# Global attention: row sums added ahead of the context tiles' scaling, and transposed behind the third pair of key tiles

## The chip, the cores and the metric

One core of a Trainium2 chip runs the whole kernel. The metric is the device time of one execution in microseconds (us), as the median of several runs. The engines are TensorE (PE for its matmuls, PEld for its weight loads), VectorE (DVE), ScalarE (ACT), GpSimd (POOL) and SyncE (SP), which issues most DMAs here.

## The reference

One transformer layer over 1024 latent tokens of width 1024, with 256 context tokens that serve as further keys. Two attention branches read the same input; what the change touches is the second, global one: 8 query heads in 2 groups of 4, each over all 1024 latent keys and the 256 context keys in one softmax.

```python
def _global_attention(q, k_all, v_all):
    def one_block(i):
        q_blk = lax.dynamic_slice_in_dim(q, i * BLOCK, BLOCK, axis=1)      # 128 queries
        p = jax.nn.softmax(_gqa_scores(q_blk, k_all), axis=-1)
        return _gqa_values(p, v_all)
...
    o_a = _windowed_attention(q_a, k_a, v_a, k_a_c, v_a_c, sink)
    o_b = _global_attention(q_b, concatenate([k_b, k_b_c]), concatenate([v_b, v_b_c]))
    y = (g_a * (o_a @ w_branch_a) + g_b * (o_b @ w_branch_b)) @ w_out
    x = _layer_norm(ALPHA * x + gate1 * y)
    x = _layer_norm(ALPHA * x + gate2 * _conv_ffn(x * (1 + scale2) + shift2))
```

All of it is in fp32.

## The kernel before, in words

fp32 is made from pairs: `split` (L79 to L86) writes a rounded high part (L81 on ACT, L83 on POOL) and a low remainder (L86), and a product is the sum of several matmuls (`mm3`, L88 to L91).

The attention runs over 32 units, first 16 of the windowed branch and then 16 of the global one. A global unit is one block of 128 queries (`i`, 0 to 7) and one group of 4 heads (`g`, 0 or 1); this text calls the unit of block 3 and group 0 "3_0". A unit has two halves.

The score half: `cxp` multiplies the queries with the 256 context keys into one score tile (s_x; L493 and L494, a matmul for the high and one for the low part), takes the row maxima on DVE (L550), scales them by the query norms (L551, 128x4), and ACT takes the exponentials (L505) into the tile p_x and their sums into smc. `lat` does the same for each of the four heads over the 1024 latent keys: scores in s_0 to s_3 (L493, L494), row maximum and copy on DVE (L538), exponentials on ACT (L505) with the sums in sm. Two score tiles have PSUM buffers at a time. Then `norm` (L558 to L573) joins both: f = exp(difference of the maxima) (L562, L563), the four 128x256 pieces of p_x are multiplied by f on POOL (L566), smc is multiplied by f (L567), and added to sm (L568).

The value half has ten key tiles, eight latent and two context ones. `tr_step` transposes each tile's four 128x128 pieces on PE into a PSUM tile ptr_n (L613), which is split into pth and ptl: by ACT (L622) and DVE (L623), or for tiles 2 and 6 by a copy on ACT (prw, L619) and both parts on POOL (L83, L86). `av_step` multiplies them with the values into the tile av (L634, L635). The context tiles, ptr_8 and ptr_9, are the only ones that read p_x. `rows` (L575 to L589) transposes sm on PE into the tile str (L577), takes the reciprocal on DVE (L581), writes it to DRAM as dn (L586) and broadcasts it back into rb by two DMAs (L588). `out_step` copies av (L640), adds its two halves on POOL (L642, L646) and multiplies by rb (L649); the split result O is read by the branch's output matmuls (L89 to L91 on tiles b), for which raw weights rwb are loaded and split into hwb and lwb (L83, L86 on POOL, L1028 for the last ones).

`value_steps` lists the steps of a unit's value half: five pairs of key tiles, with `rows` inserted between them (L666). The main loop (L964 to L996) interleaves the score half of unit u with the value half of unit u−1 and with pieces of the output products by a fraction for each step, and in some units adds weight sums: DMAs on SP (L682) that POOL's accumulating DMAs (L684) follow. From that list the framework's scheduler orders the instructions of each engine, so a step moved in the list can stand elsewhere among its neighbours on every engine. str, the ptr tiles, and the transposed queries qtr share three PSUM buffers in turn.

Of the kernel before, what the change touches and what calls it, by code (L numbers as in the profile page):

```python
# [10 lines left out]
ALU = mybir.AluOpType  # L11
# [57 lines left out]
def layer_kernel(  # L69
# [6 lines left out]
    nc = tc.nc  # L76
    PSUM = bass.MemoryType.PSUM

    def split(src, hi, lo, hi_eng, lo_eng):  # L79
        if hi_eng is nc.scalar:  # L80
            nc.scalar.copy(hi, src)  # L81
        elif hi_eng is nc.gpsimd:
            nc.gpsimd.tensor_scalar(out=hi, in0=src, scalar1=1.0, scalar2=0.0, op0=ALU.mult, op1=ALU.add)  # L83
        else:
            hi_eng.tensor_copy(hi, src)
        lo_eng.tensor_tensor(out=lo, in0=src, in1=hi.bitcast(F32), op=ALU.subtract)  # L86
# [376 lines left out]
    class Unit:  # L463
# [94 lines left out]
        def norm(self):  # L558
            hc = slice(self.g * 4, self.g * 4 + 4)
            f = small(f"f_{self.id}", (P, 4))  # L560
            if self.br:
                nc.vector.tensor_tensor(out=f, in0=self.nm, in1=self.other, op=ALU.subtract)  # L562
                nc.scalar.activation(f, f, AF.Exp)  # L563
                for h in range(4):
                    p = self.pc[h, 1]
                    nc.gpsimd.tensor_scalar(out=p, in0=p, scalar1=f[:, h:h + 1], scalar2=0.0, op0=ALU.mult, op1=ALU.add)  # L566
                nc.gpsimd.tensor_tensor(out=self.smc, in0=self.smc, in1=f, op=ALU.mult)  # L567
                nc.gpsimd.tensor_tensor(out=self.sm, in0=self.sm, in1=self.smc, op=ALU.add)  # L568
            else:
                nc.vector.tensor_tensor(out=f, in0=self.nm, in1=sinkb[:, hc], op=ALU.add)  # L570
                nc.scalar.activation(f, f, AF.Exp)
                nc.vector.tensor_tensor(out=self.sm, in0=self.sm, in1=f, op=ALU.add)
                nc.vector.reciprocal(self.sm, self.sm)  # L573
# [31 lines left out]
        def value_steps(self):  # L605
            nm, kt = self.id, self.kt
            vh = self.br * 2 + self.g
            parts = {}

            def tr_step(n):  # L610
                tr = pt_tile(f"ptr{nm}_{n}")
                for h in range(4):
                    nc.tensor.transpose(tr[:, h * P:(h + 1) * P], self.pslice(h, n), ident)  # L613
                hi = att.tile([P, 512], R32, tag="pth", name=f"pth{nm}_{n}", bufs=4)
                lo = att.tile([P, 512], R32, tag="ptl", name=f"ptl{nm}_{n}", bufs=4)
                pooled = n in POOL_LO[self.br]
                if pooled:
                    rw = att.tile([P, 512], F32, tag="ptr", name=f"prw{nm}_{n}", bufs=2)
                    nc.scalar.copy(rw, tr)  # L619
                    split(rw, hi, lo, nc.gpsimd, nc.gpsimd)  # L620
                else:
                    nc.scalar.copy(hi, tr)  # L622
                    nc.vector.tensor_tensor(out=lo, in0=tr, in1=hi.bitcast(F32), op=ALU.subtract)  # L623
                parts[n] = hi, lo
                return pooled

            def av_step(n):
                first = self.left == len(kt)
                self.left -= 1
                if first:  # L630
                    self.av = ps2.tile([P, 512], F32, tag="av", name=f"av{nm}")
                hi, lo = parts.pop(n)
                v = VT[kt[n] // 2][:, kt[n] % 2, vh]
                nc.tensor.matmul(self.av, v, hi, start=first, stop=False)  # L634
                nc.tensor.matmul(self.av, v, lo, start=False, stop=self.left == 0)  # L635

            def out_step():
                av = self.av
                avs = att.tile([P, 512], F32, tag="ptr", name=f"avs{nm}", bufs=2)
                nc.scalar.copy(avs, av)  # L640
                up = att.tile([HD, 512], F32, tag="up", name=f"up{nm}", bufs=1)
                nc.gpsimd.tensor_scalar(out=up, in0=avs[HD:P], scalar1=1.0, scalar2=0.0, op0=ALU.mult, op1=ALU.add)  # L642
                ot = att.tile([P, 2, P], F32, tag="ot", name=f"ot{nm}", bufs=1)
                oe = nc.gpsimd if self.br else nc.vector
                for h in range(2):
                    oe.tensor_tensor(out=ot[h * HD:(h + 1) * HD],  # L646
                                     in0=avs[0:HD].rearrange("p (a b q) -> p a b q", b=2, q=P)[:, :, h],
                                     in1=up.rearrange("p (a b q) -> p a b q", b=2, q=P)[:, :, h], op=ALU.add)
                nc.gpsimd.tensor_tensor(out=ot, in0=ot, in1=self.rb, op=ALU.mult)  # L649
                hf = self.i // 4  # L650
                qs = slice((self.i % 4) * P, (self.i % 4 + 1) * P)
                split(ot, otile(self.br, hf, 0, self.g)[:, :, qs], otile(self.br, hf, 1, self.g)[:, :, qs],
                      nc.gpsimd, nc.gpsimd)

            def step(ns):
                pooled = [tr_step(n) for n in ns]
                for n, pl in zip(ns, pooled):
                    clk[0] += 1
                    avq.append((self, n, clk[0] + LAG[self.br] + (PLAG[self.br] if pl else 0)))
                    av_issue()  # L660

            self.left = len(kt)
            self.av_step, self.out_step = av_step, out_step
            g = 1 + self.br
            steps = [lambda n=n: step(range(n, n + g)) for n in range(0, len(kt), g)]
            steps.insert(2 - self.br if self.br or self.i else len(steps), self.rows)  # L666
            return steps

    tokens = []
# [215 lines left out]
    def otile(br, hf, hl, g):  # L885
        key = br, hf, hl, g
        if key not in O:
            O[key] = opool.tile([P, 2, HALF], R32, tag="O", name="O%d%d%d%d" % key, bufs=12)
        return O[key]
# [4 lines left out]
    def pt_tile(name, dt=F32):  # L894
        return ps2.tile([P, 512], dt, tag="pt", name=name, bufs=3)
# [7 lines left out]
    def small(name, shape):  # L903
        return att.tile(list(shape), F32, tag=name.split("_")[0], name=name,
                        bufs=4)
# [4 lines left out]
    def av_issue(flush=False):  # L910
        while avq:
            u = avq[0][0]
            c = [e for e in avq if e[0] is u and (flush or e[2] <= clk[0])]
            if not c:
                return
            e = min(c, key=lambda e: e[2])
            avq.remove(e)
            u.av_step(e[1])
            if u.left == 0:
                u.out_step()  # L920
# [988 lines left out]
```

## Time and profile before

| | |
|---|---|
| median of 3 runs | 1570.69 us (1568.04 to 1571.46) |
| the profiled execution's own time | 1569.94 us |
| its span from first to last instruction | 1568.1 us |
| global attention in it | about 470 to 770 us of the span |
| granted TensorE clock | 0.997 of full speed on average |

A row of a timeline gives start, duration, engine, line, operation, the tiles written and read, and in brackets the idle time of the engine just ahead of it with the instruction that released it. A row of the list of waits gives the waiting engine and line, what it waited for, total idle time, how often, and the longest. A row of the groups gives busy time and mean duration in ns, then idle time ahead of them. Weight loads overlap matmuls, so the idle time ahead of a matmul (PE) and ahead of its weight load (PEld) differ.

### The profile page before, as it was taken

To read this page: it belongs to the slowest core of one execution; us is meant where nothing else is said; L and a number is where in the kernel's file an instruction comes from. 1 tells how busy PE (TensorE), PEld (TensorE's weight loads), DVE (VectorE), ACT (ScalarE), POOL (GpSimd) and SP (SyncE) were. 2 spreads that over 40 slices of the span, in tenths; PEclk is the share of its full clock that TensorE was granted. 3 is DMA by queue.
4 is the path that set the end of the run, shared out by engine and by line. 5 is a ranking of instruction groups with operands and counts; after the bars stand their busy time and mean duration, and the time that the engine had idled before them with its cause. 6 is when DMAs were issued, how large, how long until landed. Compare 5 with 4: busy or idle time off the path is not lost.

```text
span 1568.1 us, 22308 instructions
## 1 busy us (share of the span) xinstructions
PE 1532.0 (98%) x7804; PEld 1279.6 (82%) x7804; DVE 1192.3 (76%) x1707; ACT 811.3 (52%) x1430; POOL 783.6 (50%) x801
## 2 busy tenths in 40 slices
PE   9999999999999999999899999999999999999997
PEld 7888888888877777787688998888888888888887
DVE  6677976548888777778574789888888888657884
ACT  5323223358888777777330674544444444435552
POOL 0356423526667777677432444766677774021121
PEclk9999999999999999999999999999999999999998
DMA  9776662322236666430550223233334446996821
GB/s 371 266 242 237 210 247 84 112 81 63 65 123 149 155 156 168 105 86 17 179 176 27 82 93 107 96 108 109 118 111 111 112 115 188 367 266 209 254 103 55
DMA packets 113105, 232.11 MB, mean 148 GB/s; under 512 B 13056, under 2 KB 27904, under 8 KB 112896
## 3 DMA queue, kind: packets, MB, share of 16 engines
q1 hardware_dynamic: 97760, 201.82, 38.0%
q0 software_dynamic: 10400, 20.19, 8.3%
q10 hardware_dynamic: 4832, 8.68, 1.5%
q8 instruction: 61, 1.00, 0.3%
q14 instruction: 52, 0.43, 0.1%
HBM read 179.45 MB, written 65.86 MB: 156 GB/s over the span
## 4 chain that ended last, share of the span: by engine, by line
PE 84%; POOL 5%; DVE 4%; issue 2%; DMA 2%; ACT 2%; SPq 0%; DVEq 0%; ACTq 0%; POOLq 0%
PE ptr L613 5%; PE p L89 4%; PE p L90 4%; PE p L91 4%; PE g L89 4%; PE g L90 4%; PE g L91 4%; PE b L90 3%; PE b L91 3%; PE b L89 3%; PE s L493 2%; PE av L634 2%; PE av L635 2%; PE c L89 2%; PE c L91 2%; PE d L91 2%
## 5 line engine op out<-in xcount | busy, mean ns | idle before, releaser
L623 DVE TENSOR_TENSOR ptl<-ptr,pth 128x512 fp32r<-128x512 f32 x188 | 126.0, 685 | 46.5 <-ACT pth L622 43.5
L622 ACT CAST pth<-ptr 128x512 fp32r<-128x512 f32 x188 | 106.9, 588 | 55.4 <-PE av L634 25.9
L86 DVE TENSOR_TENSOR ld<-rd,hd 128x1024 fp32r<-128x1024 f32 x77 | 94.8, 1248 | 50.4 <-ACT hd L81 48.2
L505 ACT ACTIVATE p<-p,nm 128x1024 f32<-128x1024 f32 (+2 forms) x128 | 125.4, 981 | 12.0 <-DVE p L538 11.6
L613 PE MATMUL ptr<-ident,p 128*128 128x128 f32 x816 | 126.2, 277 | 2.3 <-DVE ptl L623 0.9
L81 ACT CAST hd<-rd 128x1024 fp32r<-128x1024 f32 x77 | 79.4, 1049 | 81.4 <-PE p L91 57.2
L613 PEld LDWEIGHTS ptr<-ident,p 128*128 128x128 f32 x816 | 94.6, 140 | 27.0 <-DVE ptl L623 6.3
L86 POOL TENSOR_TENSOR wlg<-wg,whg 128x512 fp32r<-128x512 f32 x32 | 47.2, 1486 | 123.6 <-ACT whg L81 84.4
L634 PE MATMUL av<-pth,VT 128*128 128x512 f32 x236 | 104.4, 442 | 1.7 <-POOL pth L83 1.2
L89 PE MATMUL p<-hd 128*128 128x512 f32 x264 | 103.3, 391 | 0.0
L90 PE MATMUL p<-ld,hd 128*128 128x512 f32 x264 | 102.8, 389 | 0.0
L91 PE MATMUL p<-hd,ld 128*128 128x512 f32 x264 | 102.8, 389 | 0.0
L635 PE MATMUL av<-ptl,VT 128*128 128x512 f32 x236 | 98.2, 416 | 3.1 <-POOL ptl L86 3.1
L89 PE MATMUL g<-hh,whg 128*128 128x512 f32 x256 | 99.9, 390 | 0.0
L91 PE MATMUL g<-hh,wlg 128*128 128x512 f32 x256 | 99.7, 389 | 0.0
L90 PE MATMUL g<-hl,whg 128*128 128x512 f32 x256 | 99.6, 389 | 0.0
L538 DVE TENSOR_SCALAR_CACHE_REDUCE p<-s,cvt,nmc 128x1024 f32<-128x1024 f32 x64 | 84.0, 1330 | 9.7 <-PE s L494 9.5
L493 PE MATMUL s<-KL,q 128*128 128x512 f32 (+2 forms) x192 | 75.4, 393 | 3.6 <-ACT p_x L505 1.8
L786 ACT ACTIVATE sg<-g,bgc 128x512 f32<-128x512 f32 x32 | 21.9, 686 | 96.1 <-PE g L91 91.3
L494 PE MATMUL s<-KL,q 128*128 128x512 f32 (+2 forms) x192 | 71.6, 373 | 0.0
L81 ACT CAST wS<-s 128x512 fp32r<-128x512 f32 x76 | 45.3, 621 | 47.5 <-POOL s L1211 46.8
L81 ACT CAST wA<-ru 128x512 fp32r<-128x512 f32 x57 | 35.5, 623 | 62.9 <-PE d L91 34.8
(436 smaller groups left out, 5022.8 us busy)
## 6 DMA issues: line engine op xcount, KB each, us to landing
wml<-in_wmodT_dram SPq DMA_DIRECT2D x48, 512.0 KB
ru<-in_w_up_dram SPq DMA_DIRECT2D x38, 512.0 KB
rd<-td SPq DMA_DIRECT2D x55, 256.0 KB
rd<-sd SPq DMA_DIRECT2D x44, 256.0 KB
rd<-in_w_dn_dram SPq DMA_DIRECT2D x33, 256.0 KB
wm<-in_wmodT_dram SPq DMA_DIRECT2D x16, 512.0 KB
wg<-in_w_g_dram SPq DMA_DIRECT2D x32, 256.0 KB
sgd<-sg ACTq DMA_DIRECT2D x32, 256.0 KB
```

What stands on the lines that cost most here:

```text
L81: nc.scalar.copy(hi, src)
L86: lo_eng.tensor_tensor(out=lo, in0=src, in1=hi.bitcast(F32), op=ALU.subtract)
L89: nc.tensor.matmul(ps, a[0], b[0], start=start, stop=False, skip_group_check=resumed)
L90: nc.tensor.matmul(ps, a[0], b[1], start=False, stop=False, skip_group_check=resumed)
L91: nc.tensor.matmul(ps, a[1], b[0], start=False, stop=stop, skip_group_check=resumed)
L493: nc.tensor.matmul(o, self.q[0][:, hs], ks, start=True, stop=False)
L505: nc.scalar.activation(p, s, AF.Exp, bias=nm[:, h:h + 1], scale=scale, accum_out=sm[:, h:h + 1])
L613: nc.tensor.transpose(tr[:, h * P:(h + 1) * P], self.pslice(h, n), ident)
L622: nc.scalar.copy(hi, tr)
L623: nc.vector.tensor_tensor(out=lo, in0=tr, in1=hi.bitcast(F32), op=ALU.subtract)
L634: nc.tensor.matmul(self.av, v, hi, start=first, stop=False)
L635: nc.tensor.matmul(self.av, v, lo, start=False, stop=self.left == 0)
```

## The change

In `norm` the two 128x4 operations on the row sums stand ahead of the four scalings of p_x (lines L564 and L565 of the changed kernel, the scaling is then L568). In `value_steps` the step `rows` goes behind the third pair of key tiles (ptr_4, ptr_5) for the 16 global units, where it stood behind the first pair (ptr_0, ptr_1). The windowed units keep their places, 2 or the end.

```diff
             if self.br:
                 nc.vector.tensor_tensor(out=f, in0=self.nm, in1=self.other, op=ALU.subtract)
                 nc.scalar.activation(f, f, AF.Exp)
+                nc.gpsimd.tensor_tensor(out=self.smc, in0=self.smc, in1=f, op=ALU.mult)
+                nc.gpsimd.tensor_tensor(out=self.sm, in0=self.sm, in1=self.smc, op=ALU.add)
                 for h in range(4):
                     p = self.pc[h, 1]
                     nc.gpsimd.tensor_scalar(out=p, in0=p, scalar1=f[:, h:h + 1], scalar2=0.0, op0=ALU.mult, op1=ALU.add)
-                nc.gpsimd.tensor_tensor(out=self.smc, in0=self.smc, in1=f, op=ALU.mult)
-                nc.gpsimd.tensor_tensor(out=self.sm, in0=self.sm, in1=self.smc, op=ALU.add)
...
             steps = [lambda n=n: step(range(n, n + g)) for n in range(0, len(kt), g)]
-            steps.insert(2 - self.br if self.br or self.i else len(steps), self.rows)
+            steps.insert(3 if self.br else 2 if self.i else len(steps), self.rows)
```

What the scheduler makes of it is shown at unit 3_0. The first place is on PE, where the score tile s_0 of unit 3_1 has just been multiplied. Before:

```order
L493 MATMUL s_3_1_0_6603<-KL_2133,q_3_1_6289 128x512
L494 MATMUL s_3_1_0_6603<-KL_2133,q_3_1_6290 128x512
L577 MATMUL str_3_0_6611<-ident,sm_3_0_6321 4x128
L613 MATMUL ptr_3_0_2_6633<-ident,p_3_0_0_6369 128x128
L613 MATMUL ptr_3_0_2_6633<-ident,p_3_0_1_6401 128x128
L613 MATMUL ptr_3_0_2_6633<-ident,p_3_0_2_6444 128x128
L613 MATMUL ptr_3_0_2_6633<-ident,p_3_0_3_6452 128x128
L634 MATMUL av_2_1_6436<-pth_2_1_9_6553,VT_2139 128x512
```

The same place after the change:

```order
L493 MATMUL s_3_1_0_6603<-KL_2133,q_3_1_6289 128x512
L494 MATMUL s_3_1_0_6603<-KL_2133,q_3_1_6290 128x512
L613 MATMUL ptr_3_0_2_6611<-ident,p_3_0_0_6369 128x128
L613 MATMUL ptr_3_0_2_6611<-ident,p_3_0_1_6428 128x128
L613 MATMUL ptr_3_0_2_6611<-ident,p_3_0_2_6456 128x128
L613 MATMUL ptr_3_0_2_6611<-ident,p_3_0_3_6464 128x128
L613 MATMUL ptr_3_0_3_6622<-ident,p_3_0_0_6369 128x128
```

str is gone from there, and the tiles ptr_2 and ptr_3 follow one another. The second place is where str stands on PE now, behind the last score tile s_3 of unit 3_1; before the change the pieces of ptr_5 stood around that tile:

```order
L493 MATMUL s_3_1_3_6688<-KL_2133,q_3_1_6289 128x512
L494 MATMUL s_3_1_3_6688<-KL_2133,q_3_1_6290 128x512
L577 MATMUL str_3_0_6696<-ident,sm_3_0_6321 4x128
L634 MATMUL av_3_0_6643<-pth_3_0_3_6627,VT_2136 128x512
L613 MATMUL ptr_3_0_6_6713<-ident,p_3_0_0_6369 128x128
L613 MATMUL ptr_3_0_6_6713<-ident,p_3_0_1_6428 128x128
```

Between the two places stand 16 transposes and 18 matmuls of 512 columns. The third place is POOL, around the scalings of p_x in the same unit. Before:

```order
L83 TENSOR_SCALAR hwb_3_0_6621<-rwb_3_0_6619 128x1024
L566 TENSOR_SCALAR p_3_0_x<-p_3_0_x,f_3_0_6475 128x256 x4
L567 TENSOR_TENSOR smc_3_0_6332<-smc_3_0_6332,f_3_0_6475 128x4
L86 TENSOR_TENSOR lwb_3_0_6622<-rwb_3_0_6619,hwb_3_0_6621 128x1024
L568 TENSOR_TENSOR sm_3_0_6321<-sm_3_0_6321,smc_3_0_6332 128x4
```

After:

```order
L83 TENSOR_SCALAR hwb_3_0_6648<-rwb_3_0_6646 128x1024
L564 TENSOR_TENSOR smc_3_0_6332<-smc_3_0_6332,f_3_0_6475 128x4
L568 TENSOR_SCALAR p_3_0_x<-p_3_0_x,f_3_0_6475 128x256
L565 TENSOR_TENSOR sm_3_0_6321<-sm_3_0_6321,smc_3_0_6332 128x4
L568 TENSOR_SCALAR p_3_0_x<-p_3_0_x,f_3_0_6475 128x256 x3
L86 TENSOR_TENSOR lwb_3_0_6649<-rwb_3_0_6646,hwb_3_0_6648 128x1024
```

The sum sm stands behind one of the four scalings, and the weight split lwb behind all of them. On DVE the reciprocal of the unit moves from behind ptl_1 to behind ptl_5, ahead of the row maximum that reads s_2 of the next unit. On SP the dn write and the two broadcasts move with it; in the last unit, 7_1, one weight load (L1028) stood between dn and the broadcasts, and now one stands ahead of dn and a second between dn and the broadcasts. Ahead of the global units and behind them the order is the same.

## The prediction

> **What bounds the kernel now.** I read the page first: span, busy shares, and the chain that ended last.
>
> ```profile
> span 1568.1 us, 22308 instructions
> PE 1532.0 (98%) x7804; PEld 1279.6 (82%) x7804; DVE 1192.3 (76%) x1707; ACT 811.3 (52%) x1430; POOL 783.6 (50%) x801
> PE 84%; POOL 5%; DVE 4%; issue 2%; DMA 2%; ACT 2%; SPq 0%; DVEq 0%; ACTq 0%; POOLq 0%
> ```
>
> TensorE (PE, with its weight loads PEld) carries 84% of that chain. The change touches only the global attention, so I then asked the windows for busy time by stage and for stretches of 20 us (columns: window, length, then busy time and count of PE, PEld, DVE, ACT, POOL, then granted clock, DMA share, GB/s).
>
> ```profile
> 470.00:770.00 300.00, 286.20 (x1628) 231.83 (x1629) 225.02 (x338) 214.01 (x454) 218.40 (x317) 1.00 0.51 124
> 590.00:610.00 20.00, 20.00 (x112) 16.52 (x113) 13.90 (x23) 14.85 (x31) 14.76 (x23) 1.00 0.64 157
> 650.00:670.00 20.00, 18.76 (x108) 15.25 (x107) 15.46 (x24) 14.47 (x31) 13.78 (x23) 1.00 0.28 57
> ```
>
> In the global stage (470 to 770) PE is busy 286.20 of 300 us at clock 1.00, while no other engine passes 232. Stretches without a stall, 590 to 610, run at 20.00 of 20. So 13.8 us of idle PE are what an edit of waits can win here. The list of waits in that window names them (total us, times, longest):
>
> ```profile
> PEld str L577 <- POOL sm L568: 11.1, 9, 1.7
> PE str L577 <- POOL sm L568: 7.2, 8, 1.2
> PEld ptr L613 <- DVE ptl L623: 4.6, 13, 0.8
> PE s L493 <- ACT p_x L505: 1.8, 3, 0.6
> PE ptr L613 <- DVE ptl L623: 1.3, 5, 0.4
> ```
>
> The largest is exactly the one the change is about: the transpose of the row sums, str, stands at the head of PE and waits for GpSimd's last addition to sm. It does so in 9 of the 16 global units.
>
> **The change part by part.** One unit shows it, 3_0 (times from the span's start, us):
>
> ```profile
> 580.04 1.85 POOL L566 TENSOR_SCALAR p_x<-p_x,f 128x256 f32<-128x256 f32 x4
> 581.86 0.20 POOL L567 TENSOR_TENSOR smc<-smc,f 128x4 f32<-128x4 f32 x1
> 582.01 2.40 POOL L86 TENSOR_TENSOR lwb<-rwb,hwb 128x1024 fp32r<-128x1024 f32 x1
> 582.20 2.22 DVE L551 TENSOR_TENSOR nmc<-nmc,cvt 128x4 f32<-128x4 f32 x1
> 583.40 0.40 PE L493 MATMUL s<-KL,q 128*128 128x512 f32 x1
> 583.63 0.40 PE L494 MATMUL s<-KL,q 128*128 128x512 f32 x1
> 584.36 0.20 POOL L568 TENSOR_TENSOR sm<-sm,smc 128x4 f32<-128x4 f32 x1
> 584.62 0.08 PEld L577 LDWEIGHTS str<-ident,sm 128*4 128x4 f32 x1 [1.03 <-POOL sm L568]
> 584.62 0.27 PE L577 MATMUL str<-ident,sm 128*4 128x128 f32 x1 [0.59 <-POOL sm L568]
> 586.80 0.50 PE L493 MATMUL s<-KL,q 128*128 128x512 f32 x1 [0.60 <-ACT p_x L505]
> ```
>
> *What a wait costs.* Two 512-wide matmuls start 0.23 us apart (583.40, 583.63), so PE's head was free at 583.86 and str began at 584.62: 0.76 us lost. The weight-load row says 1.03, the PE row 0.59. So a wait costs its weight-load gap less 0.27: 11.1 − 9 × 0.27 = 8.7 us over the stage. The bounds are the two totals, 7.2 and 11.1. By "the Trainium skill, Perfetto Trace Analysis, Identifying the Most-Contended Engine" pipelined matmuls make matmul busy time a bad measure and weight-load busy time a good one. By that page the sum would be 11.1, by PE's idle rows 7.2; the start times of unit 3_0 lie between the two, nearer to the weight loads less one matmul's pitch.
>
> *Moved on POOL.* The two 128x4 operations now run ahead of the four scalings, which took 1.85 us, and in unit 3_0 ahead of the lwb split (2.40 us), which had slipped between them. So sm is ready about 1.85 us sooner, here 4.2, and the scaled p_x about 0.4 us later (two at 0.20). p_x is first read by ptr_8, which the order puts behind six more transposed tiles: cost nothing. If that cover were gone it would be 16 × 0.4 = 6.4 us.
>
> *Moved on PE.* str goes behind ptr_5. In unit 3_0 the order puts 16 more transposes and 18 512-wide matmuls between its old place and its new one.
>
> ```profile
> 592.16 1.03 PE L613 MATMUL ptr<-ident,p 128*128 128x128 f32 x8
> 588.83 0.25 SPq L586 DMA_DIRECT2D dn<-rb  x1
> 590.01 1.29 SPq L588 DMA_DIRECT2D rb<-dn  x2
> 468.03 9.85 DMA rb<-dn
> 609.46 0.73 POOL L649 TENSOR_TENSOR ot<-ot,rb 128x256 f32<-128x256 f32 x1
> ```
>
> Eight transposes take about 0.92 of the 1.03 us at their pitch (0.115 each), so str stands 16 × 0.115 + 18 × 0.23 = 6.0 us later. Either move alone would have removed the wait: 1.85 us is over the longest wait (1.7), and 6.0 is over it by far. I take all 8.7 as removed.
>
> *Its followers.* The reciprocal, the dn write and the two rb broadcasts go 6 us later. The longest rb landing that the chain shows took 9.85 us, so rb would be there by 590.01 + 9.85 + 6.0 = 605.9; L649 multiplies by it at 609.46. Cost nothing in the middle of the stage. SP issues in order, so the q rotations and weight sums that stand behind L588 shift too. In units with a weight sum, POOL's accumulating DMA waits for SP's:
>
> ```profile
> 560.08 1.18 POOL L684 DMA_DIRECT2D sd<-in_w_dn_dram  x1 [0.41 <-DMA sd<-in_w_dn_dram]
> 569.43 0.62 POOL L83 TENSOR_SCALAR pth<-prw 128x512 fp32r<-128x512 f32 x1 [4.93 <-PE av L635]
> ```
>
> Up to 6 us of delay there meets 4.93 us of idle POOL just behind: at most 1 us of POOL in a few units, and none of it PE's. I take nothing.
>
> *What is late next.* Where the str wait goes, three units still have PE waiting for p_x of the next unit (0.6 each). That start is set by DVE's L551, which lasted 2.22 us beside POOL's lwb, and lwb follows the scalings in either order, so the gain is overtaken there, except that four transposes of ptr_3 (0.46 us) now stand ahead of it: 0.76 − 0.46 = 0.3, three times, 0.9 us given back. (lwb now comes behind sm's 0.20 too, at 582.21 at the earliest, and L551 began at 582.20; should L551 come first, these 0.9 stay a gain.) By "the Trainium skill, SBUF — State Buffer, SBUF: two separate sides" GpSimd and VectorE hold a shared port pair as an exclusive lock for a whole instruction; the trace agrees, with 2.22 us for a 128x4 operation that began 0.19 us after lwb. The other candidate is ptr waiting for ptl to free its PSUM buffer (1.3 us now): ptr_2 and ptr_3 stand closer together, and str now takes the buffer of ptr_3. I let it grow by 0.8, bounds 0 and 4.6 (the weight-load row). Net: 8.7 − 0.9 − 0.8 = 7.0 us.
>
> *The last unit.* Its rb is needed at once, and on SP the order now puts two weight loads (L1028, 128x1024 of 4 bytes, 512 KB each) ahead of the broadcasts where one stood.
>
> ```profile
> 748.57 0.27 PE L577 MATMUL str<-ident,sm 128*4 128x128 f32 x1 [0.90 <-POOL sm L568]
> 753.10 1.24 SPq L588 DMA_DIRECT2D rb<-dn  x2
> 754.39 0.59 SPq L1028 DMA_DIRECT2D rwb<-in_w_b_dram  x1
> 763.07 0.74 POOL L649 TENSOR_TENSOR ot<-ot,rb 128x256 f32<-128x256 f32 x1
> ```
>
> L588 would go out near 755 at the earliest (the second load's 0.59 and one to two us of later str), and L649 comes near 762. At a usual landing it is in time, at the longest (9.85) it is 3 us late. I take nothing and keep 3 for the range.
>
> **The rivals.** *Absorbed:* PE is released from str only to stand before ptl, p_x or a score buffer. For it: those waits sit within 2 us of str (586.80 above). Against: their PE totals, 1.8 and 1.3, are small, and the stretches without a str wait run PE at 20.00 of 20. It gives 0 ± 3 us, 1570.7. *The change does not act*, because sm was not what held str: the named releaser ended 0.06 us before the weight load in 3_0, which speaks against; also 1570.7.
>
> *Slower:* the reciprocal on DVE. Its place moves from behind ptl_1 to behind ptl_5, just ahead of the row maximum of the next unit's third score tile, and it cannot start before str, which now stands behind the fourth score tile on PE. So VectorE idles with score tiles waiting, the two score buffers come free late, and the next unit's scores wait.
>
> ```profile
> L581 DVE RECIPROCAL rb<-str 4x128 f32<-4x128 f32 x16 | 15.0, 938 | 0.4 <-PE str L577 0.4
> 527.71 1.34 DVE L538 TENSOR_SCALAR_CACHE_REDUCE p<-s,cvt,nmc 128x1024 f32<-128x1024 f32 x1 [1.36 <-PE s L494]
> ```
>
> If all 15.0 us reach PE, the balance is 15.0 − 8.7 = +6.3: 1577.0. It decides above 0.54 us a unit (8.7 / 16), and is slower by over 0.2% above 0.74. Against: str to the next unit's first score tile is 18 to 31 matmuls and transposes in the order, 3.7 to 7 us by their pitches, while str, reciprocal and row maximum take 0.27 + 0.94 + 1.34 = 2.6. Six units have only 3.7 to 4.1.
>
> **How the numbers follow.** The profiled run took 1569.94 us (span 1568.1, and 1.84 around it), 0.75 below the median of the three. 1569.94 − 7.0 = 1562.9, and with the 0.75 the median to compare is 1563.7. A difference below 0.2%, about 3.1 us, can't be told from none. Chances: forecast 0.68, its own range 1557.5 (all 11.1 us, less 2 for a median that falls as low as the lowest of the three runs, 2.65 below) to 1567.5 (half the gain lost, or the last unit's 3 us); absorbed 0.18 and not acting 0.03, together 0.21 for no change; slower by the reciprocal 0.11. The range runs to 1570.5, which takes in half of the no-change cases and leaves out the slower one.
>
> **What would show it.** Right: the waits of str on sm gone from PE and PEld, 470 to 770 of before lasting about 293 us, ptr on ptl below 3 us of PE idle, and no wait for rb at the last unit. Wrong: str gone but s on p_x, s on the row maximum or ptr on ptl grown by as much (absorbed, or slower); str still waiting (a later place on DVE or POOL sets sm); or a stage that starts at another time than 470, since everything ahead of it is in the same order.

## The result, and the profile after

The changed kernel took 1567.8 us in the median of 22 runs (1565.07 to 1570.75), the kernel before 1569.88 in 22 runs beside them. The ratio is 0.9984, with a 95% interval of 0.9978 to 0.9990: some 2.5 us faster, and inside the 0.2% that counts as no change here. The forecast was 1563.7, 7 us faster, with 0.68 on faster by more than 0.2%. The time lies 0.3 us above the forecast's own range (to 1567.5), and inside the whole range, which ran to 1570.5 because it took in half of the no-change cases.

The page and the stage window of the changed kernel, as they were shown of before:

```profile
span 1566.8 us, 22288 instructions
PE 1533.8 (98%) x7804; PEld 1283.3 (82%) x7804; DVE 1187.2 (76%) x1707; ACT 808.2 (52%) x1430; POOL 788.7 (50%) x801
...
470.00:770.00 300.00, 288.72 (x1636) 235.12 (x1636) 221.39 (x338) 212.53 (x456) 217.81 (x317) 0.99 0.51 125
```

PE's idle time in these 300 us fell from 13.8 to 11.3 us. (That is not the gain itself: from 756.7 us on, the changed kernel's trace has 3.41 us at half the clock, in which the same matmuls count as busy for longer.) The list of waits from 470 to 770 us of the changed kernel (total us, times, longest) says what filled the rest:

```profile
PEld av L634 <- ACT avs L640: 5.9, 11, 0.7
PEld s L493 <- ACT p_x L505: 5.9, 7, 1.0
PEld ptr L613 <- DVE ptl L623: 4.8, 5, 2.1
PE ptr L613 <- DVE ptl L623: 3.2, 3, 1.8
PEld av L635 <- POOL ptl L86: 3.1, 4, 1.2
PE s L493 <- ACT p_x L505: 2.8, 5, 0.6
PEld s L493 <- DVE p L538: 2.0, 3, 1.0
```

The wait of str on sm (11.1 us of weight-load idle before) is gone without a trace. In its place av waits for the copy of av's one PSUM buffer (5.9 us; 1.8 before), the scores for p_x (5.9; 3.4 before), av for POOL's ptl (3.1; 2.0) and the scores for the row maximum (2.0; 0.7). These four grew by 9.0 us together. Their rows before:

```profile
PEld s L493 <- ACT p_x L505: 3.4, 4, 1.0
...
PEld av L635 <- POOL ptl L86: 2.0, 2, 1.2
PEld av L634 <- ACT avs L640: 1.8, 8, 0.4
...
PEld s L493 <- DVE p L538: 0.7, 1, 0.7
```

The last unit is not the reason: its broadcasts went out at 753.60, sooner than the 755 that was forecast at the earliest, and L649 came 2.0 us sooner than before (761.06 against 763.07).

```profile
753.60 1.24 SPq L588 DMA_DIRECT2D rb<-dn  x2
...
761.06 0.73 POOL L649 TENSOR_TENSOR ot<-ot,rb 128x256 f32<-128x256 f32 x1
```

### The profile page after: what moved, and what is told of

It is laid out like the page before. It is cut to its first block, busy times and chain, and to the rows that moved or that the text cites. A ratio compares the mean times of both kernels' runs of the same rounds, so it can differ in the third digit from the quotient of the medians.

```text
span 1566.8 us, 22288 instructions
## 1 busy us (share of the span) xinstructions
PE 1533.8 (98%) x7804; PEld 1283.3 (82%) x7804; DVE 1187.2 (76%) x1707; ACT 808.2 (52%) x1430; POOL 788.7 (50%) x801
## 4 chain that ended last, share of the span: by engine, by line
PE 56%; DVE 2%; ACT 1%; issue 0%; POOL 0%; DVEq 0%; ACTq 0%
PE p L91 4%; PE p L89 4%; PE p L90 4%; PE b L91 3%; PE b L89 2%; PE b L90 2%; PE c L89 2%; PE a L89 2%; PE d L89 2%; PE d L91 2%; PE a L90 2%; PE c L90 2%; PE d L90 2%; PE a L91 2%; PE c L91 2%; PE y L90 2%
## 5 line engine op out<-in xcount | busy, mean ns | idle before, releaser
L613 PE MATMUL ptr<-ident,p 128*128 128x128 f32 x816 | 122.2, 276 | 4.4 <-DVE ptl L623 3.2
L493 PE MATMUL s<-KL,q 128*128 128x512 f32 (+2 forms) x192 | 75.8, 395 | 5.5 <-ACT p_x L505 2.8
```

## The experiments

Each ratio is to runs of the kernel before on the same chip; the us beside it are that ratio of 1570.

**The two halves, and the price of the wait.** Four kernels on one chip. The first has only the GpSimd half, so TensorE and VectorE keep the order of before but for one place in unit 0_0:

```diff
+                nc.gpsimd.tensor_tensor(out=self.smc, in0=self.smc, in1=f, op=ALU.mult)
+                nc.gpsimd.tensor_tensor(out=self.sm, in0=self.sm, in1=self.smc, op=ALU.add)
                 for h in range(4):
...
             steps.insert(2 - self.br if self.br or self.i else len(steps), self.rows)
```

> Only the GpSimd half of the change: the two 128x4 operations ahead of the four scalings; str stays behind the first pair, and TensorE and VectorE keep the order of the kernel before (but for one place in unit 0_0). Theory A (the wait was worth some 8 us, and str's new place gave most of it back by drawing ptr and av ahead into their own waits): the wait of str on sm all but goes, 6 to 8 us faster than before, so 4 to 6 faster than the full change. Theory B (TensorE freed from this wait stands before p_x, ptl or the next buffer in either order): 1 to 3 us faster, as the full change. Theory C (the gain was real, but a half-clock stretch at the last unit took it): 3 to 4 us faster, granted clock 0.997 or above, and no slow stretch near 757 us.

Measured: 0.9960 (0.9948 to 0.9973), 6.3 us faster. Half of the change gives two and a half times the gain of the whole, more than theory C's 3 to 4 us. Its waits from 470 to 770:

```profile
PEld ptr L613 <- DVE ptl L623: 5.8, 14, 1.0
PEld s L493 <- ACT p_x L505: 4.6, 7, 1.0
...
PEld av L634 <- ACT avs L640: 1.7, 8, 0.3
...
PEld str L577 <- POOL sm L565: 1.0, 2, 0.8
```

11.1 us of str's wait became 1.0, and the two largest others grew by 2.4 (ptr 1.2, s on p_x 1.2). So with TensorE's order unchanged the waits in the list grow little.

The second has only the other half:

```diff
-            steps.insert(2 - self.br if self.br or self.i else len(steps), self.rows)
+            steps.insert(3 if self.br else 2 if self.i else len(steps), self.rows)
```

> Only the other half: str behind the third pair, POOL in the order of before (scalings first). TensorE and VectorE stand as in the full change. Theory A and theory B both: the same as the full change, 1 to 3 us faster than before, with no wait of str on sm and the same new waits (av on avs near 5.9 us of weight-load idle, av on POOL's ptl near 4.9). If the GpSimd half mattered beside the move, it would be 1 to 2 us apart from the full change.

Measured: 0.9970 (0.9960 to 0.9981), 4.7 us faster, with the new waits of the full change (av on avs 5.8 us, s on p_x 5.5). It looks better than the full change, and its interval only just meets that one's (0.9978 to 0.9990). Whether the GpSimd half costs something beside the move stays open: within the stage the traces part by more than 0.2 us in the first interval alone (from the s_x of 0_1 to that of 1_0, see below: 0.21 us shorter than before here, 0.81 and 1.38 longer in two traces of the full change), where in the one trace a weight sum's DMA came late to GpSimd and in the other the clock went to half.

The third leaves str where it was and gives it a sum that is ready long before; it leaves the latent keys' sums out of the division:

```diff
-                nc.gpsimd.tensor_tensor(out=self.smc, in0=self.smc, in1=f, op=ALU.mult)
-                nc.gpsimd.tensor_tensor(out=self.sm, in0=self.sm, in1=self.smc, op=ALU.add)
+                nc.gpsimd.tensor_tensor(out=f, in0=self.smc, in1=f, op=ALU.mult)
+                nc.gpsimd.tensor_tensor(out=self.sm, in0=self.sm, in1=f, op=ALU.add)
...
-            nc.tensor.transpose(tr[0:4, 0:P], self.sm, ident)
+            nc.tensor.transpose(tr[0:4, 0:P], self.smc if self.br else self.sm, ident)
```

> Str stays behind the first pair and transposes the context sums smc as ACT left them, which are ready long before; the scaled sums go into f and sm and nobody reads them (the division leaves out the latent keys' sums). The wait is gone by construction, with TensorE and VectorE in the order of before. It prices the wait: theory A 7 to 9 us faster than before; theory B 1 to 3 us, with the weight-load waits of ptr on ptl and s on p_x grown from 4.6 and 3.4 us by 5 or more together.

Measured: 0.9958 (0.9946 to 0.9970), 6.6 us faster. No wait of str is left in its list, and the next ones grew little:

```profile
PEld ptr L613 <- DVE ptl L623: 4.8, 15, 0.8
PEld s L493 <- ACT p_x L505: 4.4, 7, 1.0
```

The GpSimd half alone takes nearly all of these 6.6 us. But they are not the price of the wait alone, because VectorE also moved against GpSimd. Unit 3_0 shows it: its VectorE row L551 (nmc of the next unit), 2.22 us before, now starts ahead of GpSimd's lwb and takes 0.33:

```profile
580.44 0.33 DVE L551 TENSOR_TENSOR nmc<-nmc,cvt 128x4 f32<-128x4 f32 x1
...
581.62 2.40 POOL L86 TENSOR_TENSOR lwb<-rwb,hwb 128x1024 fp32r<-128x1024 f32 x1
```

Of the 6.1 us by which this trace is shorter than before (span 1562.0 against 1568.1), 1.9 lie in the stretch around that row, from the s_x of 3_1 to that of 4_0, where str had lost no more than 0.76; with the GpSimd half it is 2.0 of 5.8. All the other waits of str together, priced at 7.9 us in the prediction (8.7 less that 0.76), gave back about 4. So theory B, that all freed time is swallowed in any order, falls, but about half of it is swallowed; and str's new place must cost some 4 us against the GpSimd half.

The fourth puts str behind the second pair (`steps.insert(2 if self.br ...`), with the GpSimd half.

> The full change with str behind the second pair of key tiles instead of the third. Theory A: the waits that the move creates are smaller, 3 to 6 us faster than before. Theory B: 1 to 3 us, as the full change. In either case no wait of str on sm above 1 us in all.

Measured: 0.9997 (0.9988 to 1.0006), no gain at all, against both theories. A single wait shows how a place can hurt: `ptr` stood 3.2 us for the reciprocal, which holds str's PSUM buffer, one of the three that the ptr tiles use too.

```profile
PEld ptr L613 <- DVE rb L581: 3.2, 1, 3.2
```

The reciprocal was late itself. It is that of unit 0_0, and in VectorE's order it stood behind L646, which had waited 3.15 us for GpSimd; that place comes back below.

**Is it str's place, or the places of the pairs?** The list of steps gives `rows` a slot of its own, so moving it also draws the second and third pair one slot ahead. Two kernels part the two; both have the GpSimd half.

```diff
+                third = steps[2]
+                steps[2] = lambda: (third(), self.rows())
+                steps.insert(1, lambda: None)
```

> The full change, but the pairs of key tiles keep the slots they had before: an empty step holds the place of str's old slot, and str runs at the end of the third pair's step. Theory D (the move costs some 4 us because the second and third pair come a slot earlier in each unit, so that av, ptr and the score tiles run into their own waits): 5 to 7 us faster than before, near the 6.3 of the GpSimd half alone, and the waits of av on avs back from 5.9 us of weight-load idle to about 2. Theory E (the cost is str's own place: its reciprocal late on VectorE ahead of a row maximum, its PSUM buffer taken between ptr_5 and ptr_6): 1 to 3 us faster, as the full change.

Measured: 1.0003 (0.9994 to 1.0013), no gain. The pairs are back in their slots, av waits for avs only 2.4 us, and still all 6.3 us are lost:

```profile
PEld ptr L613 <- DVE ptl L623: 11.7, 19, 2.2
PEld s L493 <- ACT p_x L505: 6.0, 6, 1.4
```

The opposite kernel moves the pairs and keeps str early:

```diff
+                head = steps[0]
+                steps[0] = lambda: (head(), self.rows())
+                steps.insert(3, lambda: None)
```

> The opposite: the pairs come in the slots of the full change, but str runs at the end of the first pair's step, so that it stands ahead of the next unit's first latent score tile; GpSimd's order as in the full change. Theory D: 1 to 3 us faster than before at most, av on avs near 5.9 us, and less if str, which stands even earlier here, meets its wait on sm again (up to 9 units at 1 to 2 us each). Theory E: 5 to 7 us faster, less what such a wait takes, with av on avs near 2.

Measured: 0.9974 (0.9964 to 0.9983), 4.1 us faster. Here av waits for avs 5.4 us, as in the full change, but the scores hardly wait for p_x:

```profile
PEld av L634 <- ACT avs L640: 5.4, 13, 0.7
PEld ptr L613 <- DVE ptl L623: 4.8, 9, 0.9
...
PEld s L493 <- ACT p_x L505: 0.9, 5, 0.2
```

(str waits for sm again, three times, 1.6 us, as its expectation allowed.) Theory D falls: the slots are not the cost, nor is the largest new wait in the list, av on avs. It comes with str's late place (theory E), though not through the reciprocal ahead of the row maximum alone: the scores' wait for the row maximum is 1.0 us here and 2.0 in the full change. Nor does the place cost the same in every unit: the traces of these two kernels differ by 6.1 us, and 4.5 of that lie in two intervals (2_1 to 3_0 and 3_1 to 4_0, see below), in the first of which the kernel with late str also has 3.41 us at half the clock.

On the same chip the full change was run again, and a step between (str at the end of the second pair's step, without a slot).

> The full change once more, on the chip of this call, to compare with the other runs here. All theories: 0.9978 to 0.9990 of before, that is 1.5 to 3.5 us faster; 3 us or more would say that the 4.2 us of the move without the GpSimd half were no more than this.

Measured: 0.9991 (0.9982 to 1.0001), 1.4 us faster. With the first 22 runs, the full change is worth 1 to 3 us.

> A step between: no slot of its own for str, which runs at the end of the second pair's step, so that the five pairs are spread evenly over the unit (third pair at 0.50 of it; 0.58 before, 0.42 in the full change). Theory D: between the two, 3 to 5 us faster than before. Theory E: as the run with str behind the second pair, within 1 us of before, with a wait of ptr on the reciprocal.

Measured: 0.9981 (0.9971 to 0.9990), 3.0 us faster: theory D's number, though the wait of ptr on the reciprocal that theory E foresaw is there too (2.5 us of weight-load idle, once, again behind L646 in unit 0_0). Against the run in which str had a slot behind the same pair it is 2.5 us; this run decides nothing by itself.

**Where in the stage the 4 us go.** A new look at the traces: the start of the context scores s_x of every unit (L493) divides the stage, and the kernels can be compared interval by interval, against before (us, minus is shorter):

```text
from s_x of     GpSimd half   full change   full again   0_0 kept   no lock
0_1 to 1_0         -0.86         +0.81        +1.38       -0.82      +2.33
2_1 to 3_0         -0.68         +2.05        +2.04       +2.01      -1.12
3_1 to 4_0         -1.97         -0.78        -0.77       -0.74      -2.18
6_0 to 6_1         +0.18         -0.41        -0.41       -0.40      -1.84
```

The full change loses most against the GpSimd half in the first three of these rows: 1.7 to 2.2, 2.7 and 1.2 us. In no other stretch does it lose over 0.7, and it is ahead by 0.6 to 1.1 us in four (the last row is one). (In the last column, +2.33 follows on −2.00 in the interval ahead of it.) A cost that is the same in every unit does not look like this; it points to collisions at single places. In the interval 2_1 to 3_0 the timelines (start, duration, engine) show it. First the full change:

```profile
546.45 2.83 POOL L86 TENSOR_TENSOR lwb<-rwb,hwb 128x1024 fp32r<-128x1024 f32 x1
...
546.76 2.55 DVE L551 TENSOR_TENSOR nmc<-nmc,cvt 128x4 f32<-128x4 f32 x1
...
549.34 0.56 ACT L505 ACTIVATE p_x<-s_x,nmc,cvt 128x256 f32<-128x256 f32 x1 [2.18 <-DVE nmc L551]
...
551.69 0.50 PE L493 MATMUL s<-KL,q 128*128 128x512 f32 x1 [0.59 <-ACT p_x L505]
```

And the GpSimd half alone:

```profile
544.88 0.47 DVE L551 TENSOR_TENSOR nmc<-nmc,cvt 128x4 f32<-128x4 f32 x1
...
545.39 0.56 ACT L505 ACTIVATE p_x<-s_x,nmc,cvt 128x256 f32<-128x256 f32 x1 [0.16 <-DVE nmc L551]
...
545.31 2.40 POOL L86 TENSOR_TENSOR lwb<-rwb,hwb 128x1024 fp32r<-128x1024 f32 x1
```

A product of 128x4 numbers on VectorE takes 0.47 us when it begins 0.43 us ahead of GpSimd's lwb, and 2.55 us when it begins 0.31 us behind it. Then ACT's p_x is 2 us late, s_x keeps its PSUM buffer, and the scores stand. Four units have an lwb close by: nmc is held up over 1 us in three of them before, in two with the GpSimd half, in four in the full change.

The traces of all the kernels bear this out. In the interval 3_1 to 4_0, nmc takes 0.27 to 0.48 us in four of them, and the interval is 1.7 to 2.0 us shorter than before; it takes 1.07 to 1.63 in six, with 0.7 to 1.1 us shorter; and 2.22 to 2.90 in three, with −0.1 to +0.6. In 2_1 to 3_0, leaving out the two traces that have half the clock in it, nmc of at most 0.8 us goes with 0 to 1.0 us shorter, 1.64 with 0.3 longer, and 2.5 to 2.8 with 1.6 to 2.1 longer.

In the first interval VectorE's L646, the last windowed unit's output addition, waits for GpSimd with ptl_4 behind it, and TensorE waits for ptl_4's buffer:

```profile
483.67 0.85 DVE L646 TENSOR_TENSOR ot<-avs,up 64x256 f32<-64x256 f32 x2 [3.38 <-POOL up L642]
...
485.30 0.93 PE L613 MATMUL ptr<-ident,p 128*128 128x128 f32 x5 [1.80 <-DVE ptl L623]
```

Three kernels test these two places (theory F). The first two cut lwb into four, in the full change and in the GpSimd half alone:

```diff
+                for c in range(0, 8, 2):
+                    engs[1].tensor_tensor(out=l[:, c:c + 2], in0=r[:, c:c + 2], in1=h[:, c:c + 2].bitcast(F32), op=ALU.subtract)
```

> The full change, with GpSimd's weight split lwb of the global units' fill (2.4 us, 128x1024) made in four pieces of 256 columns; all other engines in the same order. Theory F: the move costs some 4 us over the GpSimd half alone mostly because in four units VectorE's nmc (L551) now comes while lwb runs and waits for its end (2.55, 1.42, 1.42 and 1.66 us instead of 0.3), so that p_x and the next scores come late. Then no nmc lasts over 1 us, the interval from the s_x of unit 2_1 to that of 3_0 falls by 1.5 to 2.7 us, the waits of s on p_x shrink from 5.9 us of weight-load idle to below 3, and the whole is 4 to 6 us faster than before. Rival: the waits are the place's own (str, av and the buffers), and the pieces change nothing: 1.5 to 2.5 us faster than before, as the full change.

Measured: 0.9975 (0.9965 to 0.9985), 3.9 us faster: just below what theory F said, and some 1.2 us of it come ahead of the global stage, where the first lwb lies. The pieces freed nmc in two units and not in the one that costs most:

```profile
544.20 3.22 POOL L938 TENSOR_TENSOR lwb<-rwb,hwb 128x256 fp32r<-128x256 f32 x4
...
544.49 2.96 DVE L551 TENSOR_TENSOR nmc<-nmc,cvt 128x4 f32<-128x4 f32 x1
```

VectorE did not get in between the pieces there, and the interval 2_1 to 3_0 did not fall but rose, to +3.45 us; 3.41 us at half the clock from 549.9 on have a part in that. The waits of s on p_x fell from 5.9 to 3.8 us, not below 3. So this run does not settle the 2.7 us. In the next unit with an lwb nmc took 0.48 us instead of 1.42, and the interval 3_1 to 4_0 was 0.9 us shorter than in the full change. The next one is the same: 0.46 instead of 1.42, and 6_0 to 6_1 0.95 us shorter. There the lock's price is shown: an interval gives back what nmc no longer waits.

```profile
581.48 2.83 POOL L938 TENSOR_TENSOR lwb<-rwb,hwb 128x256 fp32r<-128x256 f32 x4
...
582.45 0.48 DVE L551 TENSOR_TENSOR nmc<-nmc,cvt 128x4 f32<-128x4 f32 x1
```

> The GpSimd half alone (str behind the first pair), with lwb in the same four pieces. Two of its four units still meet the lock (1.43 and 1.77 us of nmc). Theory F: 6.5 to 8 us faster than before, 0.5 to 1.5 beyond the GpSimd half alone. Rival: 6.3, the same as without the pieces.

Measured: 0.9961 (0.9949 to 0.9973), 6.1 us: nothing beyond the GpSimd half without pieces. In the unit where the pieces freed nmc (6_0, 0.47 us instead of 1.43) the interval to 6_1 is 0.93 us shorter than in the GpSimd half; the rest of the stage takes that back, and the lwb of 7_1 was not cut.

The third keeps unit 0_0 as before:

```diff
+            steps.insert((3 if self.i or self.g else 1) if self.br else 2 if self.i else len(steps), self.rows)
```

> The full change, but the first global unit 0_0 keeps str behind its first pair; the other fifteen have it behind the third. In the full change VectorE holds ptl_4 of that unit behind the last windowed unit's output addition (L646), which waits for GpSimd, and TensorE waits 2.1 us for it. If that belongs to the move's cost: the wait of 2.1 us is gone, the first interval falls by 0.7 to 1.7 us, and the whole is 3 to 4 us faster than before. Rival: the wait only moves to the next buffer, 1.5 to 2.5 us faster, as the full change.

Measured: 0.9976 (0.9967 to 0.9984), 3.8 us faster. The first interval fell from +0.81 and +1.38 to −0.82, as expected, and the 2.1 us wait is gone; from the s_x of 2_1 on the intervals are within 0.15 us of the full change's. This part of the cost, 1.6 to 2.2 us, is shown.

**Without the lock.** The last kernel adds to it another way to the context maxima, which has no VectorE operation on two SBUF tiles:

```diff
-            nc.vector.reduce_max(self.other, s.rearrange("p (a b) -> p a b", a=4), axis=AX.X)
-            nc.vector.tensor_tensor(out=self.other, in0=self.other, in1=self.qscale(nqs), op=ALU.mult)
...
+                nc.vector.tensor_scalar(out=self.pc[h, 1], in0=s[:, h * NC:(h + 1) * NC], scalar1=self.qscale(nqs)[:, h:h + 1],
+                                        scalar2=3.0e38, op0=ALU.mult, op1=ALU.min, accum_out=self.other[:, h:h + 1])
+                self.soft(self.pc[h, 1], self.pc[h, 1], h, self.other, self.smc, -1.0)
```

> The full change with unit 0_0 kept as before, and the context maxima made another way: in place of L550 and L551 (a reduction and a 128x4 product of two SBUF tiles) VectorE scales each head's scores out of PSUM into p_x and takes their minimum on the way, as L538 does for the latent scores; ScalarE's exponentials then read p_x. No VectorE operation with two SBUF tiles is left between s_x and p_x, so GpSimd's lwb has nothing to hold up there, and s_x is free once VectorE has read it. Theory F (the rest of the move's cost is nmc behind lwb, 2.7 us in the interval from the s_x of 2_1 to that of 3_0 and 0.5 to 1 in two others): that interval falls by 2 to 3 us, the waits of s on p_x (5.3 us of weight-load idle) go, and the whole is 6 to 8 us faster than before, level with the GpSimd half alone or better. Rival: the same intervals stay long by another wait (ptr on ptl, av on avs), and it stays at 3.5 to 4.5 us faster, as the run without this edit.

Measured: 0.9911 (0.9897 to 0.9925), 1556.87 us in the median, 14 us faster than before and twice what theory F said. The interval 2_1 to 3_0 went from +2.01 to −1.12, the 3 us that were expected; the two others gained 1.4 each. L646's wait for GpSimd in unit 0_0 came back here (2.95 us, with TensorE 2.6 us at ptr), which is the +2.33 of the table. In its list from 455 to 760 us no wait of the scores for ACT's p_x is left, and av on avs is down to 1.6:

```profile
PEld ptr L612 <- DVE ptl L622: 6.5, 12, 2.9
PE ptr L612 <- DVE ptl L622: 2.6, 1, 2.6
...
PEld str L576 <- POOL sm L564: 1.6, 1, 1.6
PEld av L633 <- ACT avs L639: 1.6, 7, 0.3
```

The last unit's output multiplication (L649, L648 here) starts at 748.03:

```profile
748.03 0.74 POOL L648 TENSOR_TENSOR ot<-ot,rb 128x256 f32<-128x256 f32 x1
```

lwb still ran (2.84 us in that interval), beside the last two of the four operations that took nmc's place, but all four lasted 0.47 or 0.48 us. Two things go together in this edit: nothing waits for lwb, and s_x is free when VectorE has read it, not only when ACT has made p_x of it. Which of them gives how much of the 10 us beyond the run before it was not parted. The four units with an lwb hold 8.4 of these 10 us (3.1, 1.4, 1.4, and 2.4 from the s_x of 7_1 to the last L649, where the run before it also had 3.41 us at half the clock); nmc had taken 7.1 us in them together. That speaks for the first. What is left, there and in intervals without lwb, can be the second, or the new order on TensorE that came with it.

## Why the prediction was right in sign and wrong in size

*The number.* 1567.8 lies within the stated range through the allowance for no-change cases, and not through the sum: of the 7.0 us of the sum 2.5 came, and two of its terms were wrong by several us.

*What bounds the kernel.* Right: TensorE's idle time in the global stage was the prize, and str's wait for sm its largest piece.

*The price of the wait.* 8.7 us, less what later waits take back, 7.0 net. The two kernels in which the wait goes and TensorE's order stays measured 6.3 and 6.6 us, which looks like a term that holds. It was partly luck: some 2 us of each came in the one interval in which nmc got ahead of lwb, a shift that the prediction did not expect there (it gave 0.3 us for that unit), and the other waits gave about 4 of the 7.9 us that they were priced at. The weight-load idle, 11.1, was farther off still. The Trainium skill, Perfetto Trace Analysis, Identifying the Most-Contended Engine, names weight-load busy time as a measure of how near TensorE is to its limit; to price a wait by it was the prediction's own step, and the runs do not bear that out.

*Either move alone removes it.* Right for both: 1.0 us of weight-load idle is left with the GpSimd half, none with the other.

*Moved on PE.* This is the step that failed: str's 6 us on the way to its new place were priced by its followers (rb, dn, the weight sums, the last unit), each of which was in time, and so at nothing. With str late the change is worth some 4 us less than the GpSimd half alone. With the pairs' slots kept and str late the gain is 0; with the pairs moved and str early it is 4.1; in the change as made about 2. The cost sits at a few places: against the GpSimd half 2.7 and 1.2 us in the two intervals where nmc met lwb, and 1.7 to 2.2 where L646 held up ptl_4; elsewhere the change gained and lost smaller amounts. With str late, the PSUM buffers turn in another order, the reciprocal stands elsewhere on VectorE, and VectorE and GpSimd shift against one another; by which of these str's place brings the collisions about was not parted further. The sum had no term for any.

*What is late next.* 1.7 us were given back in the sum; some 4 us more is what the runs show. The mechanism was named for three units, nmc beside lwb, and taken as the same in either order, with the note that a start 0.01 us apart would decide. It decides indeed, but in another unit: in 2_1, where before nmc came 0.26 us ahead of lwb and took 0.16 us (its rows of before are these), it now comes 0.31 behind and takes 2.55.

```profile
546.63 0.16 DVE L551 TENSOR_TENSOR nmc<-nmc,cvt 128x4 f32<-128x4 f32 x1
...
546.89 2.38 POOL L86 TENSOR_TENSOR lwb<-rwb,hwb 128x1024 fp32r<-128x1024 f32 x1
```

The price per unit was put at 0.3; it was 2.7 in this one. The Trainium skill, SBUF — State Buffer, SBUF: two separate sides, gives the rule (an exclusive lock of the shared port pair for a whole instruction); the trace agrees, with 2.55 us against 0.16. L646 in unit 0_0 was not seen at all. That av on avs would grow from 1.8 to 5.9 us was not seen either, and cost little: the kernel with str early has it at 5.4 and is 4.1 us faster.

*The rivals.* "Absorbed" came closest by its number, but only half by its reason: when only the wait goes, about half of the freed time is kept. It was held unlikely because the totals of the other waits were small before; how large a wait is before says little of how large it becomes when the engines shift. "Slower by the reciprocal" saw a real thing: VectorE now stands 6.0 us for str at the reciprocal (0.4 before). It reached TensorE only in part, 1.3 us more of scores waiting for the row maximum.

```profile
L581 DVE RECIPROCAL rb<-str 4x128 f32<-4x128 f32 x16 | 15.1, 941 | 6.0 <-PE str L577 6.0
```

## What to carry to other kernels

When a wait can be removed by making its operand sooner, do that and leave the order alone: here the two operations moved up on GpSimd were worth 6.3 us, and moving the waiting instruction as well gave 4 of them back. Before moving a step in a list that a scheduler interleaves, look for a VectorE operation on two SBUF tiles that starts close to a long GpSimd operation: here a shift of 0.6 us turned 0.16 us into 2.55, at single places that no total shows. Compare two kernels interval by interval before believing the list of waits; its largest new entry was not the cost.

## What the hardware did that was not expected

The same program's runs differ by the clock that TensorE was granted: of 22 runs of the changed kernel the fastest, 1565.07 us, had 0.998 and the slowest, 1570.75, had 0.994. In the traces the clock goes to half for 3.41 us at a time, at places that change between runs: in the repeat of the full change at 484.8 us, just behind the 2.1 us for which TensorE stood for ptl; in the first profile not there but at 756.7. Windows of 4 us around these (the granted clock is the third number from the end):

```profile
484.00:488.00 4.00, 3.85 (x19) 3.37 (x20) 4.00 (x8) 1.76 (x3) 3.66 (x6) 0.60 0.34 61
```

```profile
756.00:760.00 4.00, 4.00 (x11) 3.12 (x12) 0.00 (x0) 0.59 (x1) 1.13 (x2) 0.59 0.92 319
```

In the second, matmuls of 512 columns start 0.43 us apart instead of 0.23, so that a stretch costs up to 1.6 us of dense work (3.41 × 0.2 / 0.43). The kernel before has such runs too (0.994 to 0.998), so much of this is spread. Whether the move adds to it is open: the granted clock averages 0.9955 over the 34 runs of the full change and 0.9965 over the 6 of the GpSimd half, and 0.001 of 1568 us is some 1.5 us; and a stretch begins between 753 and 761 us in seven of the eight traces of kernels with str behind the third pair or the pairs moved up, in none of the other six. Within one trace the starts lie whole multiples of 3.413 us apart (756.69 and 855.68: 29 of them). Those before 700 us stand at waits of TensorE of 1.4 to 2.7 us, but the wait of 1.80 us at 485.30 in the first profile has none beside it. That a stall of TensorE brings the half clock on was not tested.

Cutting a long GpSimd operation into pieces is no sure way past it for a VectorE that waits: in one unit nmc waited 2.96 us through all four pieces, in the next 0.48 through less than one (rows above). In the first the pieces overlap, 1.17 us each and started 0.70 apart behind a DMA that GpSimd issued; in the second each takes 0.74. Whether that set the two apart was not tested.
